# Token scaling on one core: seven token groups re-cut to one of 14 and six of 19, and the per-token weights brought in as long rows and spread to the partitions by TensorE transposes

## The chip, the cores and the metric

The kernel runs on 1 core of one Trainium2 chip. The metric is the device time of one execution in microseconds (us). Three executions of the kernel before were timed; the median counts.

## The reference, cut to what matters

```python
batch, seq, hidden, k = 16, 1024, 512, 2
x_expanded = x[:, :, np.newaxis, :].repeat(k, axis=2)      # x: (16, 1024, 512) float32
return x_expanded * expert_weights[..., np.newaxis]        # weights: (16, 1024, 2) float32
```

Each of 16,384 tokens has a row of 512 numbers and two weights. The output holds the row twice, once times each weight. The expert indices are not used. So 32 MiB are read, 64 MiB are written, and one multiplication is done for each number written. The weights are 128 KiB in all.

## The kernel before

The tokens are cut into seven groups. A group of T tokens per partition covers 128·T consecutive tokens, and partition p holds T consecutive tokens of it, so that a load of x moves one contiguous row of T·2 KB to each partition, and a store of the output one contiguous row of 4 KB for each token that it holds. The groups are 19, 19, 18, 18, 18, 18 and 18 tokens (line 30).

All x loads are issued from ScalarE's queue (line 77), all stores from SyncE's queue (line 117). There are two x buffers (`x_pool`) and three output buffers (`o_pool`). Each group is worked off in two halves (`halves`): the first takes the odd token, so 10 and 9 tokens or 9 and 9. For each half, `products` has VectorE multiply all tokens but the last in one instruction (line 85), with x broadcast over the two weights and the weights broadcast over the 512 numbers, while ScalarE does the two products of the last token (line 98). Then the half is stored. After both halves, the load of the group after next is issued, since it needs this group's x buffer. Group 0's x is loaded in its two halves, so that work can begin with the first; the others are loaded whole.

The weights lie in one tile, `w_tile`, 128 partitions by 256 numbers, for the whole kernel. They come by three DMAs (`weights`, line 50): group 0's from SyncE's queue, group 1's and then those of groups 2 to 6 together from ScalarE's queue, behind the two half loads of group 0 and ahead of the load of group 1. Each writes, for each partition and group, one run of T·2 numbers: 152 bytes for 19 tokens, 144 bytes for 18. That makes 128 + 128 + 640 = 896 such rows.

The order is the program's own (`manual_schedule`); nothing is reordered.

Of the kernel before, what the change touches and what calls it, by code (L numbers as in the profile page):

```python
# [1 line left out]

# [4 lines left out]


@with_exitstack
def kernel(  # L10
    ctx: ExitStack,
    tc: tile.TileContext,
    x: bass.AP,
    expert_indices: bass.AP,
    expert_weights: bass.AP,
    out: bass.AP,
):
    nc = tc.nc

    batch, seq, hidden = x.shape  # L20
    k = expert_weights.shape[-1]
    P = nc.NUM_PARTITIONS
    ntok = batch * seq
    assert ntok % P == 0

    f32 = mybir.dt.float32
    row = k * hidden


    groups = [19, 19, 18, 18, 18, 18, 18]  # L30
    assert sum(groups) * P == ntok
    TX = max(groups)
    TO = (TX + 1) // 2

    xf = x.rearrange("b s h -> (b s) h")
    of = out.rearrange("b s k h -> (b s) (k h)")
    wf = expert_weights.rearrange("b s k -> (b s) k")

    w_pool = ctx.enter_context(tc.tile_pool(name="w_pool", bufs=1))
    x_pool = ctx.enter_context(tc.tile_pool(name="x_pool", bufs=2))  # L40
    o_pool = ctx.enter_context(tc.tile_pool(name="o_pool", bufs=3))

    w_tile = w_pool.tile([P, sum(groups) * k], f32)

    def rows(flat, done, T):
        return flat[done * P : (done + T) * P, :].rearrange("(p a) n -> p (a n)", a=T)

    def weights(eng, head, G, T):
        lo = head * P
        eng.dma_start(  # L50
            out=w_tile[:, head * k : (head + G * T) * k].rearrange(
                "p (g n) -> p g n", g=G
            ),
            in_=wf[lo : lo + G * T * P, :].rearrange(
                "(g p a) n -> p g (a n)", g=G, p=P
            ),
        )

    ctx.enter_context(tc.manual_schedule())

    starts = [sum(groups[:i]) for i in range(len(groups))]
    loaded = []


    def halves(i):
        T = groups[i]
        return [T - T // 2, T // 2]

    def load(i):
        if i >= len(groups):  # L70
            return
        x_tile = x_pool.tile([P, TX * hidden], f32)
        loaded.append(x_tile)
        src = rows(xf, starts[i], groups[i])
        lo = 0
        for n in halves(i) if i == 0 else [groups[i]]:
            nc.scalar.dma_start(
                out=x_tile[:, lo * hidden : (lo + n) * hidden],
                in_=src[:, lo * hidden : (lo + n) * hidden],
            )  # L80
            lo += n

    def products(o_tile, x_tile, at, n, w_at):
        m = n - 1
        nc.vector.tensor_tensor(  # L85
            out=o_tile[:, : m * row].rearrange("p (t k h) -> p t k h", t=m, k=k),
            in0=x_tile[:, at * hidden : (at + m) * hidden]
            .rearrange("p (t h) -> p t h", t=m)
            .unsqueeze(2)
            .to_broadcast([P, m, k, hidden]),  # L90
            in1=w_tile[:, w_at : w_at + m * k]
            .rearrange("p (t k) -> p t k", t=m)
            .unsqueeze(3)
            .to_broadcast([P, m, k, hidden]),
            op=mybir.AluOpType.mult,
        )
        for c in range(m * k, n * k):
            nc.scalar.mul(  # L98
                out=o_tile[:, c * hidden : (c + 1) * hidden],
                in_=x_tile[:, (at + c // k) * hidden : (at + c // k + 1) * hidden],  # L100
                mul=w_tile[:, w_at + c : w_at + c + 1],
            )

    weights(nc.sync, 0, 1, groups[0])
    load(0)
    weights(nc.scalar, starts[1], 1, 19)
    weights(nc.scalar, starts[2], 5, 18)
    load(1)

    for i, T in enumerate(groups):  # L110
        x_tile = loaded[i]
        outr = rows(of, starts[i], T)
        at = 0
        for n in halves(i):
            o_tile = o_pool.tile([P, TO * row], f32)
            products(o_tile, x_tile, at, n, (starts[i] + at) * k)
            nc.sync.dma_start(  # L117
                out=outr[:, at * row : (at + n) * row], in_=o_tile[:, : n * row]
            )
            at += n  # L120
        load(i + 2)

# [1 line left out]
_INS = ['x', 'expert_indices', 'expert_weights']  # L124
_OUTS = [((16, 1024, 2, 512), 'float32')]


# [23 lines left out]
```

## Time and profile before

| | |
|---|---|
| timed runs | 239.56, 239.70, 240.71 us; median 239.7 us |
| the profiled execution | 239.73 us in all, span 237.9 us from first to last instruction |
| bytes moved by DMA | 100.80 MB, mean 424 GB/s over the span |
| VectorE busy | 123.7 us (52%), 14 instructions |
| ScalarE busy | 20.0 us (8%), 29 instructions |
| GpSimd busy | 0.2 us; TensorE is not used |
| DMA packets | 4112 |

Engines are named as in the profile: PE is TensorE, DVE is VectorE, ACT is ScalarE, POOL is GpSimd, SP is SyncE; ACTq and SPq are the queues from which DMAs are issued (q10 is ScalarE's, q1 SyncE's in the table of queues). In the views by window, the columns are the window, its length, each engine's busy time with its number of instructions, the granted TensorE clock, the mean busy share of the 16 DMA engines, and GB/s. A packet is counted whole in the window in which it starts, so a short window's share can be over 1.

### The profile page before, as it was taken

The numbers are of one execution on the slowest core, as the hardware profiler recorded it, in microseconds if no ns is written. First come the engines' busy times: TensorE is split into PE (matmuls) and PEld (weight loads), VectorE is DVE, ScalarE is ACT, GpSimd is POOL, SyncE is SP. The second block draws the span as 40 slices with busy tenths as digits, with TensorE's granted clock in tenths as the row PEclk, the third lists the DMA queues.
The fourth block names the chain that finished last, engine by engine and source line by source line (L and its number), as shares of the span: only waits on it lengthen the run. The fifth ranks groups of instructions, "written<-read, shape, count | busy, mean of one in ns | idle before, by whom it ended". The sixth has DMA issues, their size and how long they took to land.

```text
span 237.9 us, 159 instructions
## 1 busy us (share of the span) xinstructions
DVE 123.7 (52%) x14; ACT 20.0 (8%) x29; POOL 0.2 (0%) x4
## 2 busy tenths in 40 slices
DVE  0499659293193077950494900769505949680000
ACT  2220020100100020200202000202002020200000
POOL 0000000000000000000000000000000000000000
DMA  7999999999999999999999999999999999999996
GB/s 275 420 446 347 430 430 431 476 415 409 495 419 419 430 403 484 403 415 477 397 446 446 397 477 415 409 484 397 434 459 397 477 415 403 490 397 422 471 397 298
DMA packets 4112, 100.80 MB, mean 424 GB/s; under 512 B 1296, under 2 KB 1296, under 8 KB 1296
## 3 DMA queue, kind: packets, MB, share of 16 engines
q1 hardware_dynamic: 2160, 67.13, 65.4%
q10 hardware_dynamic: 1952, 33.67, 33.5%
HBM read 33.69 MB, written 67.11 MB: 424 GB/s over the span
## 4 chain that ended last, share of the span: by engine, by line
DMA 67%; DVE 22%; issue 0%; DVEq 0%; SPq 0%
DMA out_dram<-o_tile 63%; DVE o_tile L85 22%; DMA x_tile<-in_x_dram 4%; DVEq L85 0%; SPq L117 0%
## 5 line engine op out<-in xcount | busy, mean ns | idle before, releaser
L85 DVE TENSOR_TENSOR o_tile<-x_tile,w_tile 128x8192 f32<-128x8192 f32 (+1 forms) x14 | 123.7, 8844 | 89.4 <-DMA out_dram<-o_tile 75.4
L98 ACT ACTIVATE o_tile<-x_tile,w_tile 128x512 f32<-128x512 f32 x28 | 18.7, 714 | 181.7 <-DMA out_dram<-o_tile 157.4
L98 ACT ACT_TABLE_LOAD x1 | 1.3, 1283 | 4.2 <-DMA w_tile<-in_expert_weights_dram 4.2
L135 POOL MEMSET const-bfloat16-1.0<- 128x1 bf16 x1 | 0.1, 101 | 0.0
L135 POOL MEMSET const-uint8-127<- 128x1 uint8 x1 | 0.1, 101 | 0.0
L135 POOL MEMSET const-float32-0.0<- 128x1 f32 x1 | 0.1, 98 | 0.2 <-issue 0.2
L135 POOL MEMSET const-float32-1.0<- 128x1 f32 x1 | 0.1, 98 | 0.0
## 6 DMA issues: line engine op xcount, KB each, us to landing
out_dram<-o_tile SPq DMA_DIRECT2D x12, 4608.0 KB, 35.4
x_tile<-in_x_dram ACTq DMA_DIRECT2D x5, 4608.0 KB, 26.1
out_dram<-o_tile SPq DMA_DIRECT2D x2, 5120.0 KB, 34.8
x_tile<-in_x_dram ACTq DMA_DIRECT2D x1, 4864.0 KB, 29.5
x_tile<-in_x_dram ACTq DMA_DIRECT2D x1, 2560.0 KB, 8.8
x_tile<-in_x_dram ACTq DMA_DIRECT2D x1, 2304.0 KB, 13.9
w_tile<-in_expert_weights_dram ACTq DMA_DIRECT2D x1, 90.0 KB, 13.6
w_tile<-in_expert_weights_dram SPq DMA_DIRECT2D x1, 19.0 KB, 3.4
```

Source lines behind the costliest of these rows:

```text
L85: nc.vector.tensor_tensor(out=o_tile[:, : m * row].rearrange("p (t k h) -> p t k h", t=m, k=k), in0=x_tile[:, at * hidden : (at + m) * hidden]
L98: nc.scalar.mul(out=o_tile[:, c * hidden : (c + 1) * hidden], in_=x_tile[:, (at + c // k) * hidden : (at + c // k + 1) * hidden], mul=w_ti ...
L135: nc = _bacc.Bacc("TRN2", target_bir_lowering=False, num_devices=1)
```

## The change

The groups become 14, 19, 19, 19, 19, 19 and 19 tokens, so the first two stores hold 7 tokens each and all later ones 10 or 9. The number of x loads (8) and of stores (14) is the same.

The weights come in two DMAs (`weights_in`). One row of such a DMA is the weights of B = 8 partitions in a row: 8·14·2 numbers, 896 bytes, on 16 partitions for group 0; 8·19·2 numbers, 1216 bytes, on 96 partitions for the six other groups together. `weights_columns` then spreads them. For each of the 8 partitions r in a row, TensorE transposes that row's slice, so that tokens' weights lie on the partitions and (group, partition) on the free axis; VectorE copies the results out of PSUM, four slices at a time, in the order of the partitions; then TensorE transposes each group's 128 columns back, which gives 128 partitions by T·2 numbers, and `weights_out` copies these to `w_tile`. For group 0 that is 8 + 1 transposes and 2 + 1 copies, ahead of everything else on VectorE. For the other six groups it is 8 + 6 transposes and 2 + 1 copies; the two copies stand between VectorE's first and second product of group 0, the last one behind the second product. The transposes need an identity matrix, which GpSimd makes with a memset and an affine select.

```diff
-    groups = [19, 19, 18, 18, 18, 18, 18]
+    groups = [14, 19, 19, 19, 19, 19, 19]
...
+    B = 8
+    M = P // B
+    ident = w_pool.tile([P, P], f32)
+    nc.gpsimd.memset(ident, 0.0)
+    nc.gpsimd.affine_select(
+        out=ident,
+        in_=ident,
+        compare_op=mybir.AluOpType.not_equal,
+        fill=1.0,
+        base=0,
+        pattern=[[-1, P]],
+        channel_multiplier=1,
+    )
+
+    def weights_in(eng, head, G, T):
+        raw_tile = raw_pool.tile([G * M, B * T * k], f32, name=f"raw{T}_tile")
         eng.dma_start(
-            out=w_tile[:, head * k : (head + G * T) * k].rearrange(
-                "p (g n) -> p g n", g=G
+            out=raw_tile,
+            in_=wf[head * P : (head + G * T) * P, :].rearrange(
+                "(q a) n -> q (a n)", a=B * T
             ),
-            in_=wf[lo : lo + G * T * P, :].rearrange(
-                "(g p a) n -> p g (a n)", g=G, p=P
-            ),
+        )
+        return raw_tile
+
+    def weights_columns(raw_tile, G, T):
+        n = T * k
+        col_tile = raw_pool.tile([n, G * P], f32, name=f"col{T}_tile")
+        cols = col_tile.rearrange("c (q r) -> c q r", r=B)
+        for r0 in range(0, B, B // 2):
+            up_tile = psum.tile([n, B // 2, G * M], f32)
+            for r in range(B // 2):
+                nc.tensor.transpose(
+                    up_tile[:, r, :],
+                    raw_tile[:, (r0 + r) * n : (r0 + r + 1) * n],
+                    ident[: G * M, : G * M],
+                )
+            nc.vector.tensor_copy(
+                out=cols[:, :, r0 : r0 + B // 2],
+                in_=up_tile.rearrange("c r q -> c q r"),
+            )
+        down_tile = psum.tile([P, G * n], f32)
+        for g in range(G):
+            nc.tensor.transpose(
+                down_tile[:, g * n : (g + 1) * n],
+                col_tile[:, g * P : (g + 1) * P],
+                ident[:n, :n],
+            )
+        return down_tile
+
+    def weights_out(down_tile, head, G, T):
+        nc.vector.tensor_copy(
+            out=w_tile[:, head * k : (head + G * T) * k], in_=down_tile
         )
...
-    weights(nc.sync, 0, 1, groups[0])
+    raw_a = weights_in(nc.sync, starts[0], 1, 14)
     load(0)
-    weights(nc.scalar, starts[1], 1, 19)
-    weights(nc.scalar, starts[2], 5, 18)
+    raw_b = weights_in(nc.scalar, starts[1], 6, 19)
     load(1)
+    weights_out(weights_columns(raw_a, 1, 14), starts[0], 1, 14)
...
-        for n in halves(i):
+        for j, n in enumerate(halves(i)):
+            if i == 0 and j == 1:
+                down_b = weights_columns(raw_b, 6, 19)
             o_tile = o_pool.tile([P, TO * row], f32)
             products(o_tile, x_tile, at, n, (starts[i] + at) * k)
...
             at += n
+        if i == 0:
+            weights_out(down_b, starts[1], 6, 19)
         load(i + 2)
```

More of the change, by code (lines that the diff above doesn't have):

```diff
@@ L46, in rows @@
         return flat[done * P : (done + T) * P, :].rearrange("(p a) n -> p (a n)", a=T)
-    def weights(eng, head, G, T):
-        lo = head * P
+    B = 8
[13 more added lines that the diff above has]
+        raw_tile = raw_pool.tile([G * M, B * T * k], f32, name=f"raw{T}_tile")
         eng.dma_start(
-            out=w_tile[:, head * k : (head + G * T) * k].rearrange(
-                "p (g n) -> p g n", g=G
-            ),
-            in_=wf[lo : lo + G * T * P, :].rearrange(
-                "(g p a) n -> p g (a n)", g=G, p=P
-            ),
+            out=raw_tile,
+            in_=wf[head * P : (head + G * T) * P, :].rearrange(
+                "(q a) n -> q (a n)", a=B * T
+            ),
+        )
[22 more added lines that the diff above has]
+                ident[:n, :n],
+            )
+        return down_tile
+    def weights_out(down_tile, head, G, T):
+        nc.vector.tensor_copy(
+            out=w_tile[:, head * k : (head + G * T) * k], in_=down_tile
         )
```

3 lines of the change are left out of this document (added).

## The prediction

> **What bounds the kernel now.** I read the profile page first, for who is busy and what the chain that ended last is made of.
>
> ```profile
> span 237.9 us, 159 instructions
> DVE 123.7 (52%) x14; ACT 20.0 (8%) x29; POOL 0.2 (0%) x4
> DMA  7999999999999999999999999999999999999996
> DMA packets 4112, 100.80 MB, mean 424 GB/s; under 512 B 1296, under 2 KB 1296, under 8 KB 1296
> DMA out_dram<-o_tile 63%; DVE o_tile L85 22%; DMA x_tile<-in_x_dram 4%; DVEq L85 0%; SPq L117 0%
> ```
>
> No engine is busy for more than half the span, while the DMA line shows a 9 in every slice but the first and the last. The chain names VectorE's products with 22%, but DMA is full while they run, so that share is no bound. The waits say the same from the other side:
>
> ```profile
> ACT o_tile L98 <- DMA out_dram<-o_tile: 157.4, 11, 20.2
> DVE o_tile L85 <- DMA out_dram<-o_tile: 75.4, 11, 12.9
> DVE o_tile L85 <- DMA x_tile<-in_x_dram: 14.0, 2, 9.5
> ```
>
> Eleven of the fourteen products wait for an output buffer whose store has not landed. So I asked for the DMA rate by stretch:
>
> ```profile
> 1.90:2.60 0.70, 0.00 (x0) 0.00 (x0) 0.00 (x0) 1.00 0.64 189
> 4.50:9.00 4.50, 0.00 (x0) 0.96 (x1) 0.00 (x0) 1.00 1.00 430
> ...
> 15.40:22.00 6.60, 6.60 (x2) 1.06 (x2) 0.00 (x0) 1.00 1.01 413
> 24.50:213.00 188.50, 108.55 (x13) 16.01 (x24) 0.00 (x0) 1.00 1.00 432
> 213.00:236.90 23.90, 0.18 (x1) 0.00 (x0) 0.00 (x0) 1.00 0.97 420
> 236.90:237.90 1.00, 0.00 (x0) 0.00 (x0) 0.00 (x0) 1.00 0.00 0
> ```
>
> The middle 188.5 us run at 432 GB/s with a share of 1.00. At that rate 100.80 MB take 233.3 us. Nothing moves in the first 1.9 us or the last 1.0 us. 237.9 − 233.3 − 1.9 − 1.0 leaves 1.7 us that are lost near the start. The change moves the same x and output bytes, so these 1.7 us are all that it can win; the rest it could only lose. The profiled execution took 239.73 us, 1.83 us more than its span; the median is 239.7 us, so a difference in span can be taken from either.
>
> **The cost of small weight rows.** The weights are 896 rows of 144 or 152 bytes. Of the 1296 packets under 512 B the other 400 are what 25 DMAs leave at 16 each, and 4112 − 1296 = 2816 is 22 loads and stores of 128 rows. The window from 14.0 to 14.6 us, in which the second and third weight DMA run, gives the price of one:
>
> ```profile
> DMA packets 503, 0.19 MB, mean 309 GB/s; under 512 B 500, under 2 KB 500, under 8 KB 500
> q10 hardware_dynamic: 503, 0.19, 118.6%
> ```
>
> 118.6% of 16 engines for 0.6 us is 11.4 engine-us. Three of the packets are x rows of 38 KB, which at 432/16 = 27 GB/s take 1.44 us each, 4.3 together. The other 500 take 7.1, so 14.2 ns each. 896 of these are 12.7 engine-us, 0.80 us on each of 16 engines. This lies on the path, since the engines have no idle time to hide it.
>
> The change has 16 rows of 896 bytes and 96 of 1216, so 1 and 6 for each engine if the rows are spread evenly. I price each at 14.2 ns and its additional bytes at 27 GB/s: (896 − 146)/27 = 28 ns more, so 42 ns; (1216 − 146)/27 = 40 ns more, so 54 ns. 42 + 6 × 54 is 0.37 us for each engine. The gain is 0.80 − 0.37 = **0.43 us**. It could be 0.2 where small rows partly overlap their neighbours, as a share over 100% allows.
>
> At the start, 1.90 to 2.60 runs at 189 GB/s instead of 432, which loses 0.7 × 243/432 = 0.39 us. In it x's first rows and group 0's 128 weight rows start together, from two queues. The weight rows fall to 16. Between nothing (the queues ramp up by themselves) and 0.39 I take half, **0.2 us**.
>
> A rule speaks for more. The Trainium skill, "DMA: Bandwidth & Descriptors", section "Specifications", wants at least 512 bytes for line rate and says that below this the DMA engine does a read-modify-write. The row above gives 14.2 ns for a 146-byte row, 9 ns more than its bytes at 27 GB/s, so in the packet's own time the trace shows little of that; what is left of it would have to sit outside the records, which is the second rival below.
>
> **Tiles of 7, 10 and 9 tokens.** Loads stay 8 and stores 14, all of 128 rows, so the number of large rows stays 2816 and their bytes too: no change. Rows of 38 KB (x of 19 tokens) and 40 KB (10 tokens out) exist already in groups 0 and 1.
>
> **The work added on the engines** costs nothing as long as DMA never runs out of issued transfers. The one place where it might is the first stores.
>
> ```profile
> 0.72 0.89 ACTq L77 DMA_DIRECT2D x_tile<-in_x_dram  x2
> 0.72 0.37 SPq L50 DMA_DIRECT2D w_tile<-in_expert_weights_dram  x1
> 1.64 1.17 ACTq L50 DMA_DIRECT2D w_tile<-in_expert_weights_dram  x2
> 2.84 0.60 ACTq L77 DMA_DIRECT2D x_tile<-in_x_dram  x1
> 9.50 18.36 DVE L85 TENSOR_TENSOR o_tile<-x_tile,w_tile 128x9216 f32<-128x9216 f32 x2 [9.50 <-DMA x_tile<-in_x_dram]
> 19.35 194.23 SPq L117 DMA_DIRECT2D out_dram<-o_tile  x14
> ```
> ```profile
> L85 DVE TENSOR_TENSOR o_tile<-x_tile,w_tile 128x8192 f32<-128x8192 f32 x12 | 104.3, 8692 | 75.4 <-DMA out_dram<-o_tile 75.4
> L85 DVE TENSOR_TENSOR o_tile<-x_tile,w_tile 128x9216 f32<-128x9216 f32 x2 | 19.5, 9758 | 14.0 <-DMA x_tile<-in_x_dram 14.0
> L98 ACT ACTIVATE o_tile<-x_tile,w_tile 128x512 f32<-128x512 f32 x28 | 18.7, 714 | 181.7 <-DMA out_dram<-o_tile 157.4 <-DMA x_tile<-in_x_dram 24.3
> L135 POOL MEMSET const-float32-0.0<- 128x1 f32 x1 | 0.1, 98 | 0.2 <-issue 0.2
> ```
> ```profile
> x_tile<-in_x_dram ACTq DMA_DIRECT2D x1, 4864.0 KB, 29.5
> x_tile<-in_x_dram ACTq DMA_DIRECT2D x1, 2560.0 KB, 8.8
> w_tile<-in_expert_weights_dram ACTq DMA_DIRECT2D x1, 90.0 KB, 13.6
> w_tile<-in_expert_weights_dram SPq DMA_DIRECT2D x1, 19.0 KB, 3.4
> ```
>
> When the reads run out: the change first loads 14 + 19 tokens, 3584 + 4864 KB, and 128 KB of weights: 8576 KB or 8.78 MB, at 430 GB/s 20.4 us. From 1.9 us and 0.7 for the slow beginning, they end at 23.0. From issue (0.72) to first packets (1.9) it is 1.2 us, so the first store has to be issued by 21.8.
>
> When the first store is issued: its x is 1792 KB instead of 2560, 0.79 MB or 1.8 us less, so it is there at 9.50 − 1.8 = 7.7. Its weights land by 0.72 + 3.4 = 4.1. Then 9 transposes and 3 copies follow one another. No row shows TensorE; the nearest are a memset of one number per partition, 0.1 us, and an ACTIVATE of 512 numbers, 0.71. The pieces have 16 to 128 columns, so 12 × 0.1 = 1.2 us to 12 × 0.71 = 8.6 us; I take 0.3 us each, 3.6 us, since they lie between these two sizes and have hand-overs. The weights are then ready at 7.7 (5.3 to 12.7), about with x. GpSimd's two instructions for the identity, at 0.1 to 0.71 each, are done before the weights land. The product of 6 tokens has 6144 numbers; by (9758 − 8692)/1024 = 1.04 ns per number it takes 8692 − 2132 = 6560 ns. The store is issued at 14.3, at worst 19.3; before it was 19.35. The margin to 21.8 is 7.5, at worst 2.5 us.
>
> The second store: the two copies of group 1 to 6 stand on VectorE ahead of the second product, and that product, the second store and the load of group 2 (which waits for the buffer) queue behind them. The raw rows landed 13.6 us after an issue at 1.64 to 2.8, behind 4864 KB of x; behind 3584 KB it is 3.0 us sooner, by 13.4. Eight transposes at most 0.71 each: 19.1, mostly beside the first product. Two copies and 6.56 us: the store is issued at about 21.5, at worst 27.3. The reads and the first store (3.67 MB, 8.5 us) last to 31.5, so it is needed by 30.3. The six transposes back run beside that product, and the last copy delays group 1's product by under 0.71. Group 1's x lands at the latest with the 31.5, its product is done at 42, and by then the second store and group 2's load have put 20 us more in the queue. From there a group costs VectorE 9.76 + 8.69 = 18.5 us and DMA 14.94 MB, 34.6 us. On SP nothing but stores follows the weights; ScalarE issues one DMA less ahead of group 1's load, and finds the queue full either way. The end is as before: the last product has 9 tokens, and two stores are queued behind each other.
>
> Sum: 239.73 − 0.43 − 0.2 = **239.1 us**, a span of 237.3.
>
> **The rivals.** *Small rows cost more than their records show.* Then most of the 1.7 us goes, and about 1.5 with it: 238.2 us. For it: the low rate sits where small rows run, and the rule above. Against it: the same stretch holds the ramp of the queues and the first store's arrival, which stay.
>
> *Rows of 38 KB are slower.* In 15.4 to 22.0 only group 1's x is read, at 413 GB/s against 430 at 4.5 to 9.0. If that is the rows' own rate, five more such loads, 24.9 MB, take 60.3 instead of 57.9 us: 239.1 + 2.4 = 241.5 us. Against it: a packet is counted where it starts, and one round of 16 packets is 0.62 MB of the 2.7 in that window. It decides from a true rate under some 418 GB/s, where the loss is over 1.7 us.
>
> *The weights come too late and DMA starves.* If a step of the chain takes 1.5 us instead of 0.3, it ends at 4.1 + 18 = 22.1, the first store reaches the engines at 22.1 + 6.6 + 1.2 = 29.9 instead of by 23.0, and the time is 246. It begins to cost where the first product starts after 15.2. Against it: the bound from rows is 12.7.
>
> *The change does not do what it says:* the weight DMAs weigh as much as before, or were beside other work. Then it is 239.7, within the forecast's own side.
>
> **How the numbers follow.** About 0.5%, 1.2 us, is what can be told from no change: 238.5 to 240.9. The forecast with its bounds (gain of 0.2 to 0.8) and the rival of no effect have 0.76, all within; the faster rival 0.13; the two slower ones 0.07 and 0.04. So faster 0.13, same 0.76, slower 0.11. The range reaches from the faster rival, 238.2, to what one of the runs before reached, 240.7, with a part of the slow rows in it.
>
> **What would show it.** The profile after should have a 9 in all slices but the ends, 4112 − 896 + 112 − 16 = 3312 packets (one DMA less, so 384 under 512 B, and 112 more under 2 KB), the first product at about 7.7 (up to 12.7) and the first store at about 14.3, and 432 GB/s again from 24.5 on. The forecast is wrong if a stretch between 3 and 236 us shows DMA idle, if the rate with 38 KB rows falls below 430, or if the span shrinks by more than 1.2 us, which would say that small rows cost what their records do not show.

## The result: 1% slower, and the profile after

The changed kernel takes 242.67 us in the median of 19 runs (240.15 to 243.89), the kernel before 239.84 us (239.51 to 241.94, 19 runs). The ratio is 1.0093, 95% interval 1.0069 to 1.0117, from the comparisons, which leave disturbed runs out already. The forecast was 239.1 us, "same"; the range ended at 240.7. By the prediction's own bound of 0.5% this is slower, to which it gave a chance of 0.11. The profiled execution took 241.77 us, with a span of 240.0.

The page after, its span, its DMA lines and its chain:

```profile
span 240.0 us, 217 instructions
DMA  6998999999999999999999999999999999999992
GB/s 246 476 417 372 437 439 453 424 453 426 426 432 416 473 429 419 432 423 394 479 428 439 426 417 399 494 425 432 426 407 436 474 423 431 393 433 430 466 430 123
DMA packets 3312, 100.80 MB, mean 420 GB/s; under 512 B 384, under 2 KB 496, under 8 KB 496
DMA out_dram<-o_tile 64%; DVE o_tile L136 21%; DMA x_tile<-in_x_dram 3%; DVE col_tile L92 0%; DVEq L136 0%; SPq L170 0%
```

The packets are as worked out: 3312, 384 and 496. DMA is as full as before in all slices but one near the start and the ends, and the chain has the same members and, for under 1%, two copies of the weights. What differs is the last slice: 2 tenths and 123 GB/s, where before it was 6 tenths and 298.

The same stretches as in the prediction, in the changed kernel (engines PE, PEld, DVE, ACT, POOL, then clock, DMA share, GB/s):

```profile
1.90:2.60 0.70, 0.00 (x0) 0.00 (x0) 0.00 (x0) 0.00 (x0) 0.00 (x0) 1.00 0.65 131
4.50:9.00 4.50, 0.00 (x0) 0.00 (x0) 1.05 (x2) 0.89 (x1) 0.00 (x0) 1.00 1.00 424
15.40:22.00 6.60, 0.85 (x6) 0.71 (x6) 6.60 (x2) 0.00 (x0) 0.00 (x0) 1.00 1.00 413
24.50:213.00 188.50, 0.00 (x0) 0.00 (x0) 109.48 (x12) 16.01 (x24) 0.00 (x0) 1.00 1.00 432
213.00:236.90 23.90, 0.00 (x0) 0.00 (x0) 1.13 (x1) 0.00 (x0) 0.00 (x0) 1.00 0.96 416
```

The middle runs at 432 GB/s, as before. So the loss is at neither the rate nor the issue. It is in the last three microseconds. Before, then after, by single microseconds:

```profile
235.00:236.00 1.00, 0.00 (x0) 0.00 (x0) 0.00 (x0) 1.00 1.02 442
236.00:237.00 1.00, 0.00 (x0) 0.00 (x0) 0.00 (x0) 1.00 0.01 0
237.00:238.00 1.00, 0.00 (x0) 0.00 (x0) 0.00 (x0) 1.00 0.00 0
```
```profile
235.00:236.00 1.00, 0.00 (x0) 0.00 (x0) 0.00 (x0) 0.00 (x0) 0.00 (x0) 1.00 0.26 111
236.00:237.00 1.00, 0.00 (x0) 0.00 (x0) 0.00 (x0) 0.00 (x0) 0.00 (x0) 1.00 0.18 74
237.00:238.00 1.00, 0.00 (x0) 0.00 (x0) 0.00 (x0) 0.00 (x0) 0.00 (x0) 1.00 0.09 37
238.00:239.00 1.00, 0.00 (x0) 0.00 (x0) 0.00 (x0) 0.00 (x0) 0.00 (x0) 1.00 0.00 0
```

A packet counts where it starts. Before, the last rows start ahead of 236, and none after. In the changed kernel 74 GB/s for one microsecond is 74 KB, two rows of 36,864 bytes, and 37 is one row, between 237 and 238. Most of the 16 DMA engines have finished, while a few still have a row to move. The last store has landed only when the last engine is done.

The trace also has the time at which each of the 16 engines reports its share of a DMA as landed. In the change, thirteen engines have landed the last store by 236.75 us, two more by 237.8, and one at 239.16. For each kernel the table gives the first and the last of these times, from its profiled execution, with the time that the first store was issued. The variants, e1 to e15, are described below. The ratios go by the kernel before as it was timed beside each variant; its median there was 240.27 us (e1 to e4), 240.34 (e5 to e8), 239.87 (e9 to e11) and 240.39 (e12 to e15), so the medians of these four sets are not to be compared with each other.

| kernel | first store issued, us | first engine done, us | last engine done, us | median, us | ratio to before, 95% interval |
|---|---|---|---|---|---|
| before | 19.35 | 236.55 | 237.01 | 239.84 | |
| the change | 14.78 | 236.30 | 239.16 | 242.67 | 1.0093 (1.0069 to 1.0117) |
| e1, new groups alone | 14.46 | 236.20 | 239.50 | 242.43 | 1.0074 (1.0039 to 1.0110) |
| e2, long weight rows alone | 19.42 | 236.30 | 236.65 | 240.58 | 1.0008 (0.9979 to 1.0037) |
| e3, 20 and six 18, long rows | 19.46 | 236.33 | 237.59 | 240.19 | 1.0000 (0.9976 to 1.0025) |
| e4, 20 and six 18, small rows | 19.60 | 236.41 | 237.54 | 240.09 | 1.0004 (0.9984 to 1.0023) |
| e5, six 19, then 14 | 19.13 | 236.42 | 236.87 | 239.77 | 0.9994 (0.9952 to 1.0035) |
| e6, 14 first, then even | 14.43 | 236.48 | 238.15 | 242.01 | 1.0062 (1.0026 to 1.0098) |
| e7, stores of 10 and 8 | 19.41 | 236.39 | 239.17 | 240.78 | 1.0021 (0.9987 to 1.0056) |
| e8, change, group 0 as 10 and 4 | 19.41 | 236.02 | 237.34 | 240.86 | 1.0029 (0.9997 to 1.0061) |
| e9, change, first store held | 18.94 | 236.01 | 240.07 | 240.85 | 1.0024 (0.9990 to 1.0059) |
| e10, before, group 0 as 7, 6, 6 | 14.36 | 236.70 | 240.77 | 243.04 | 1.0084 (1.0046 to 1.0122) |
| e11, before, first store held | 23.80 | 236.32 | 237.65 | 240.82 | 1.0027 (0.9991 to 1.0064) |
| e12, change, one queue | 15.17 | 236.66 | 241.07 | 243.08 | 1.0099 (1.0061 to 1.0138) |
| e13, before, one queue | 19.97 | 236.71 | 239.90 | 242.50 | 1.0065 (1.0037 to 1.0092) |
| e14, 7, 6, 6 and held | 18.70 | 236.53 | 239.48 | 241.25 | 1.0035 (1.0007 to 1.0063) |
| e15, long weight rows, one queue | 19.75 | 236.85 | 239.78 | 242.79 | 1.0089 (1.0056 to 1.0123) |

In every kernel the first engine is done between 236.0 and 236.9 us, and the span ends 0.81 to 0.99 us after the last engine. What differs is how far the last engine lags: 0.46 us before, 2.86 us in the change. The 2.1 us by which the span grew are this lag (2.4 us more) less 0.25 us by which the first engine ended sooner. A single execution says little of a kernel, since the lag differs from run to run (before ranges from 239.51 to 241.94, and the profiled executions of e9 and e14, 242.67 and 242.24 us, are among the longest of theirs); the ratios and intervals carry the comparisons below.

### The profile page after: what moved, and what is told of

The parts are those of the page before. It is cut to its first block, busy times and chain, and to the rows that moved or that the text cites. A ratio compares the mean times of both kernels' runs of the same rounds, so it can differ in the third digit from the quotient of the medians.

```text
span 240.0 us, 217 instructions
## 1 busy us (share of the span) xinstructions
PE 3.0 (1%) x23; PEld 2.2 (1%) x23; DVE 125.4 (52%) x20; ACT 20.0 (8%) x29; POOL 0.7 (0%) x6
## 2 busy tenths in 40 slices
DMA packets 3312, 100.80 MB, mean 420 GB/s; under 512 B 384, under 2 KB 496, under 8 KB 496
## 4 chain that ended last, share of the span: by engine, by line
DMA 67%; DVE 21%; issue 0%; DVEq 0%; SPq 0%
DMA out_dram<-o_tile 64%; DVE o_tile L136 21%; DMA x_tile<-in_x_dram 3%; DVE col_tile L92 0%; DVEq L136 0%; SPq L170 0%
## 5 line engine op out<-in xcount | busy, mean ns | idle before, releaser
L136 DVE TENSOR_TENSOR o_tile<-x_tile,w_tile 128x9216 f32<-128x9216 f32 (+2 forms) x14 | 123.7, 8842 | 84.6 <-DMA out_dram<-o_tile 73.2
L92 DVE COPY col_tile<-up_tile 28x64 f32<-28x64 f32 (+1 forms) x4 | 1.3, 374 | 3.8 <-PE up_tile L87 3.8
L87 PE MATMUL up_tile<-ident,raw_tile 16*28 16x16 f32 (+1 forms) x16 | 1.8, 269 | 12.1 <-DMA raw_tile<-in_expert_weights_dram 12.1
L87 PEld LDWEIGHTS up_tile<-ident,raw_tile 16*28 16x28 f32 (+1 forms) x16 | 1.3, 119 | 12.3 <-issue 12.2
L98 PE MATMUL down_tile<-ident,col_tile 38*128 38x38 f32 (+1 forms) x7 | 1.2, 305 | 1.4 <-DVE col_tile L92 1.4
L98 PEld LDWEIGHTS down_tile<-ident,col_tile 38*128 38x128 f32 (+1 forms) x7 | 0.9, 208 | 1.9 <-DVE col_tile L92 1.9
L106 DVE COPY w_tile<-down_tile 128x28 f32<-128x28 f32 (+1 forms) x2 | 0.6, 284 | 0.4 <-PE down_tile L98 0.4
```

Source lines behind the costliest of these rows:

```text
L87: nc.tensor.transpose(up_tile[:, r, :], raw_tile[:, (r0 + r) * n : (r0 + r + 1) * n], ident[: G * M, : G * M],)
L92: nc.vector.tensor_copy(out=cols[:, :, r0 : r0 + B // 2], in_=up_tile.rearrange("c r q -> c q r"),)
L98: nc.tensor.transpose(down_tile[:, g * n : (g + 1) * n], col_tile[:, g * P : (g + 1) * P], ident[:n, :n],)
L106: nc.vector.tensor_copy(out=w_tile[:, head * k : (head + G * T) * k], in_=down_tile)
L136: nc.vector.tensor_tensor(out=o_tile[:, : m * row].rearrange("p (t k h) -> p t k h", t=m, k=k), in0=x_tile[:, at * hidden : (at + m) * hidden]
```

## The experiments

**Which half of the change?** The groups were changed without the weights (e1), and the weights without the groups (e2).

```diff
e1, in the kernel before:
-    groups = [19, 19, 18, 18, 18, 18, 18]
+    groups = [14, 19, 19, 19, 19, 19, 19]
...
-    weights(nc.scalar, starts[1], 1, 19)
-    weights(nc.scalar, starts[2], 5, 18)
+    weights(nc.scalar, starts[1], 6, 19)
e2, in the changed kernel (columns and copies likewise):
-    groups = [14, 19, 19, 19, 19, 19, 19]
+    groups = [19, 19, 18, 18, 18, 18, 18]
...
-    raw_b = weights_in(nc.scalar, starts[1], 6, 19)
+    raw_c = weights_in(nc.scalar, starts[1], 1, 19)
+    raw_b = weights_in(nc.scalar, starts[2], 5, 18)
```

> The changed groups (14 and six times 19) with the three-row-size small weight DMAs of before (two DMAs, rows of 112 and 152 bytes). Theory P (the group cut makes DMA engines drift apart: its stores alternate between rows of 40 and 36 KB and its loads have 38 KB, where before nearly all rows had 36 KB, so an engine that falls behind stays behind and the last store ends on one late engine): slow like the change, 241.5 to 243 us (ratio 1.007 to 1.013), one or a few engines with their last packets 1 to 3 us after the others. Theory W (the long weight rows upset the start, 16 rows on 16 engines and 6 each, and the spread seeded there stays): like before, 239.5 to 240.3 us, all engines ending within 0.7 us.

> The groups of before (19, 19, five times 18) with the weights in long rows and TensorE transposes (rows of 1216, 1216 and 1152 bytes). Theory P (group cut): like before or 0.3 to 0.6 us less, 239.1 to 239.8 us, engines ending within 0.7 us. Theory W (weight rows): slow like the change, 241.5 to 243 us, a late engine at the end.

e1 is as slow as the change, 1.0074, and e2 is like before, 1.0008 with an interval that reaches to both sides. So theory W falls: the groups do it, and the weights show neither harm nor gain. The end of e1 and that of e2, in the same single microseconds:

```profile
236.00:237.00 1.00, 0.00 (x0) 0.00 (x0) 0.00 (x0) 1.00 0.26 111
237.00:238.00 1.00, 0.00 (x0) 0.00 (x0) 0.00 (x0) 1.00 0.34 147
```
```profile
236.00:237.00 1.00, 0.00 (x0) 0.00 (x0) 0.00 (x0) 0.00 (x0) 0.00 (x0) 1.00 0.01 0
237.00:238.00 1.00, 0.00 (x0) 0.00 (x0) 0.00 (x0) 0.00 (x0) 0.00 (x0) 1.00 0.00 0
```

e1 has rows left that start after 237 us, with small weight rows; e2 has none after 236, with long ones.

**Long against small weight rows with even groups** (e3 and e4: 20 and six times 18; otherwise as the changed kernel, and as the kernel before).

> Groups of 20 and six times 18, so all halves equal (10 and 10, then 9 and 9; rows of 36 KB for nearly all loads and stores), with the weights in long rows and transposes. Theory P: 239.0 to 239.8 us, the engines together at the end. Theory W: 241.5 to 243 us. A third theory, F (it is the early first store of the group of 14, with x rows of 14 KB, that upsets the engines): like before here, and slow in the run with the groups alone.

> Groups of 20 and six times 18 with the small weight rows of before. Theory P and F: like before, 239.5 to 240.2 us. Theory W: like before too. Beside the run with the long rows it gives the price of the small rows by itself: 0.43 us by the prediction.

Both are like before (1.0000 and 1.0004). They are 0.1 us apart, by the medians the wrong way round and by the ratios the right way, so the 0.43 us of the small rows can't be seen here, nor ruled out. The long rows are not worth over about 0.5 us, the edge of e2's interval (0.21% of 239.8).

**Unequal rows through the run, or the early first store?** The new groups have two properties: stores of 40 and 36 KB rows beside loads of 38 KB, and a first group so small that its first store comes at 14.8 us. e5 keeps the first and takes away the second, e6 the reverse; e7 adds unequal stores to the kernel before; e8 gives the changed kernel's first store 10 tokens.

```diff
e5, in the kernel before (weights cut likewise):
-    groups = [19, 19, 18, 18, 18, 18, 18]
+    groups = [19, 19, 19, 19, 19, 19, 14]
e6, in the kernel before (weights cut likewise):
-    groups = [19, 19, 18, 18, 18, 18, 18]
+    groups = [14, 20, 20, 20, 18, 18, 18]
e7, in the kernel before:
-        return [T - T // 2, T // 2]
+        return [10, T - 10]
e8, in the changed kernel:
-        return [T - T // 2, T // 2]
+        return [10, 4] if i == 0 else [T - T // 2, T // 2]
```

> Six groups of 19 and 14 last, small weight rows. The first two groups, the first store and the x loads beside it are those of before; from the third group on loads have rows of 38 KB and stores of 40 and 36 KB. Theory P (unequal rows make engines drift apart through the run): 241.5 to 243 us. Theory F (the first store of a small first group comes at 15 us, in the middle of the x loads, and seeds the lag): like before, 239.5 to 240.5 us.

> Groups of 14, 20, 20, 20, 18, 18, 18, small weight rows: the small first group of the change, but all halves equal and loads and stores of one row size in each group (40 KB, then 36 KB). Theory P: like before, 239.5 to 240.5 us. Theory F: 241.5 to 243 us.

> The kernel before with its 18-token groups stored as 10 and 8 tokens instead of 9 and 9 (rows of 40 and 32 KB; loads stay 36 KB). Theory P: slower than before by 1 to 3 us. Theory F: like before, 239.5 to 240.5 us.

> The changed kernel with group 0 cut into 10 and 4 tokens instead of 7 and 7, so that the first store is issued at about 19.3 us as before, not at 14.8; all else stays. Theory F: 239.5 to 240.5 us, like before. Theory P: 241.5 to 243 us, as the change.

e5, the same seven sizes with the 14 at the end, is like before (0.9994); e6, with even halves but 14 first, is slow (1.0062). That is theory F and against P. e7 is not distinguishable from before (1.0021). e8 falls from 1.0093 to 1.0029, a little above what F expected in the median, 240.86 us. The rows of 38 KB, one of the prediction's rivals, are cleared by e5 as well: it has five such loads where before has one and the change six, no loss, and this rate in the middle:

```profile
24.50:213.00 188.50, 105.77 (x13) 16.01 (x24) 0.00 (x0) 1.00 1.00 433
```

**Is it the time of the first store, or the small pieces?** In e9 and e11 VectorE does the product of the first four tokens twice, which holds the first store back by 4.2 to 4.5 us. What VectorE does behind it, the other stores of group 0 and the load of group 2 come as much later too. e10 cuts the 19 tokens of group 0 of the kernel before into 7, 6 and 6, so that its first store comes early; e14 is e10 with the store held back.

```diff
e9, e11 and e14:
+            if i == 0 and at == 0:
+                twice(o_tile, x_tile, 0)
             products(o_tile, x_tile, at, n, (starts[i] + at) * k)
e10 and e14, in the kernel before:
-        return [T - T // 2, T // 2]
+        return [7, 6, 6] if i == 0 else [T - T // 2, T // 2]
```

> The changed kernel, in which VectorE does the product of the first four tokens of the first tile twice (4096 numbers, about 4.3 us), so that the first store is issued at about 19.1 us instead of 14.8; nothing else differs. Theory F1 (the time of the first store, in the middle of the x loads, makes an engine late): back to 239.5 to 240.8 us, near before. Theory F2 (it is the small group itself, its 14 and 28 KB rows): stays at 242 to 243 us.

> The kernel before with group 0 (19 tokens) loaded and stored as 7, 6 and 6 tokens instead of 10 and 9: the first store is issued at about 14.5 us, with one load and one store more. Theory F1: slower than before by 1.5 to 2.5 us, 241.5 to 243. Theory F2 (a small group): like before, 239.5 to 240.5.

> The kernel before with the same doubled product: the first store is issued at about 23.6 us instead of 19.35, shortly before the reads run out at about 26. Theory F1: like before or with fewer late engines, 239.5 to 239.9 us median, and 240.5 to 242 if the reads run out first. Theory F2: like before.

> The kernel before with group 0 loaded and stored as 7, 6 and 6 tokens and the product of the first four tokens done twice, so that the first store is issued at about 18.8 us instead of 14.4. Theory F1 (the time of the first store): 239.7 to 241 us, 2 us less than with the three pieces alone. Theory F2 (small pieces at the start): 242.4 to 243.5, as with the three pieces alone.

The timelines of SyncE's queue in e10, e9 and e14 show that the stores of group 0 moved as a whole, with the distance between them as it was (in the change the two begin at 14.78 and take 7.70):

```profile
14.36 11.11 SPq L117 DMA_DIRECT2D out_dram<-o_tile  x3
```
```profile
18.94 7.71 SPq L187 DMA_DIRECT2D out_dram<-o_tile  x2
```
```profile
18.70 11.11 SPq L134 DMA_DIRECT2D out_dram<-o_tile  x3
```

Making the first store early in the kernel before costs 0.84%, 2 us (e10; by the medians of its set it is 3.2 us). Holding it back takes most of the loss away in both: 1.0093 to 1.0024 in the changed kernel, with intervals that do not overlap, and 1.0084 to 1.0035 in the cut one, where they do. VectorE does 4.4 us more work in these faster kernels. F1 carries the larger part, though e9, e10 and e14 each came out up to 0.25 us above the range that it gave, and e11 0.9 us above. Each pair spans two sets, so its two ratios go by different timings of the kernel before. Of what moves with the first store, the load of group 2 does not look like the cause: e8 issues it at 23.59 us, 1.4 us later than the change, and is rid of most of the loss, while e10 issues it at 25.16 and is slow. That the small pieces have a part of their own, some 0.25%, is possible: e8, e9 and e14 all lie between 1.0024 and 1.0035, but only e14's interval is clear of 1. Holding back further does not help: e11, which has no small pieces and its first store at 23.8 us, is 1.0027, with an interval from 0.9991 to 1.0064.

The end of e10, whose late engines still begin rows between 238 and 239:

```profile
236.00:237.00 1.00, 0.00 (x0) 0.00 (x0) 0.00 (x0) 1.00 0.35 148
237.00:238.00 1.00, 0.00 (x0) 0.00 (x0) 0.00 (x0) 1.00 0.17 74
238.00:239.00 1.00, 0.00 (x0) 0.00 (x0) 0.00 (x0) 1.00 0.26 111
```

**Why does an engine fall behind?** A thought was that each DMA engine serves a row of the load queue and a row of the store queue in turn, and that this lets them part. In e12, e13 and e15 all DMAs are issued from SyncE's queue, in the same program order.

```diff
-            nc.scalar.dma_start(
+            nc.sync.dma_start(
...
-    raw_b = weights_in(nc.scalar, starts[1], 6, 19)
+    raw_b = weights_in(nc.sync, starts[1], 6, 19)
```

> The changed kernel with its x loads and raw weights issued from SyncE's queue too, in the same program order, so that each DMA engine serves loads and stores one DMA after another and not a row of each in turn. Theory Q (an engine falls behind where it has two queues to serve in turn): no late engine, 238.8 to 239.6 us, faster than the change by about 3 us. Theory M (it falls behind because some engines read while others write, whatever the queue): 241.5 to 243 us, as the change. If DMA ran out of issued work, over 243.

> The kernel before with all DMAs on SyncE's queue, same program order. Theory Q: 239.3 to 239.7 us in nearly all runs, without the runs of 241 to 242 that before has. Theory M: like before, 239.5 to 242 us.

> The groups of before, the weights in long rows with transposes, all DMAs on SyncE's queue: a candidate to beat both. By theory Q 238.9 to 239.4 us, before less the 0.4 us of the small rows; by theory M 239.5 to 242 us.

Theory Q falls. e12 takes 243.08 us (1.0099, 1.0061 to 1.0138), e13 242.50 us (1.0065, 1.0037 to 1.0092), e15 242.79 us (1.0089, 1.0056 to 1.0123). One queue makes the kernel before slow too. DMA does not run out; in e13 the middle runs at 431 GB/s and the end shows a late engine, as in the change:

```profile
24.50:213.00 188.50, 106.19 (x13) 16.00 (x24) 0.00 (x0) 1.00 1.00 431
...
236.00:237.00 1.00, 0.00 (x0) 0.00 (x0) 0.00 (x0) 1.00 0.26 111
237.00:238.00 1.00, 0.00 (x0) 0.00 (x0) 0.00 (x0) 1.00 0.00 0
238.00:239.00 1.00, 0.00 (x0) 0.00 (x0) 0.00 (x0) 1.00 0.09 37
```

By the landing times of e13's DMAs, the engines are 0.5 us apart at 85 us, 1.35 at 96, 2.4 at 130 and 3.2 at the end. There the lag is not one event but grows in steps. That would fit theory M, that an engine which reads while the others write, or the reverse, loses more; but M expected e13 and e15 within 239.5 to 242 us, and both are slower. It stays open.

One thing that the traces do show is how the first store meets the loads. Before, then the change:

```profile
22.00:23.00 1.00, 1.00 (x1) 0.00 (x0) 0.00 (x0) 1.00 1.42 389
23.00:24.00 1.00, 1.00 (x1) 0.00 (x0) 0.00 (x0) 1.00 0.00 0
24.00:25.00 1.00, 1.00 (x1) 0.00 (x0) 0.00 (x0) 1.00 1.51 655
```
```profile
17.00:18.00 1.00, 0.00 (x0) 0.00 (x0) 1.00 (x1) 0.00 (x0) 0.00 (x0) 1.00 1.44 545
18.00:19.00 1.00, 0.00 (x0) 0.00 (x0) 1.00 (x1) 0.00 (x0) 0.00 (x0) 1.00 0.18 68
19.00:20.00 1.00, 0.00 (x0) 0.00 (x0) 1.00 (x1) 0.00 (x0) 0.00 (x0) 1.00 1.10 469
```

Before, no row starts on any engine for a whole microsecond: in the packet records the 38 KB rows then under way take 2.1 to 2.4 us instead of 1.44, on all 16 engines, and all engines go on together. In the change rows do start in that time, and those under way take up to 0.4 us longer, each by another amount. It is tempting to say that the common hold keeps the engines together, but the traces speak against it. In e11 the first store's rows start at 26.1 us as the loads end, no row is held, and the engines land group 1's load within 0.6 us of each other. In e9 only some rows are held, by up to 0.4 us, and the engines land that load within 0.54 us.

Nor is the lag of the change there from the first store on. At 30 us its engines land group 1's load 2.2 us apart (before, at 32 us, 0.5), but up to a row of the store, 1.06 us, of this can be the order in which an engine took its two queues. At 87 us, when stores alone have been under way for some ten us, they are 1.1 us apart (before, in such a stretch at 95, 0.5). At 124, again with stores alone, they are 2.8 apart, as at the end. In between the load issued at 85.83 us begins beside the stores, and single rows are slow: one store row of 40 KB that starts at 89.0 takes 2.4 us where others take 1.51, and two rows of the load at 107 and 108 take 0.5 and 0.6 us more than their 1.44. In e1 four store rows that start at 88.7 to 89.1 take 3.0 us, and its engines go from 0.8 us apart at 87 to 3.1 at 124; e10 has four such rows, of 2.5 to 2.6 us, at 67.4. After 26 us, before, e2, e3, e4 and e5 have no row of 28 KB or more that takes over 0.5 us more than is usual for its size and queue, and theirs are the smallest lags of all, 0.35 to 1.26 us; each of the other kernels has three or more. So the lag of these executions is made in the middle of the run; that the slow rows make it is likely, and not shown. How the time of the first store bears on them stays open: e9 and e14, with the store held, have such rows too.

## Why the prediction was wrong, point by point

The step that failed is the one that costed the earlier first store at nothing: "The work added on the engines costs nothing as long as DMA never runs out of issued transfers", and with it "The end is as before". DMA did not run out, and the times in that part lay within their bounds or ahead of them: the first product started at 8.13 us (forecast 7.7, up to 12.7), the first store was issued at 14.78 (14.3, up to 19.3), as this part of the timeline after and the line for SyncE's stores show.

```profile
3.44 0.29 PEld L87 LDWEIGHTS up_tile<-ident,raw_tile 16*28 16x28 f32 x8 [3.44 <-issue]
...
4.51 0.19 DVE L106 COPY w_tile<-down_tile 128x28 f32<-128x28 f32 x1 [0.40 <-PE down_tile L98]
8.11 1.28 ACT L149 ACT_TABLE_LOAD   x1 [8.11 <-DMA x_tile<-in_x_dram]
8.13 6.56 DVE L136 TENSOR_TENSOR o_tile<-x_tile,w_tile 128x6144 f32<-128x6144 f32 x1 [3.44 <-DMA x_tile<-in_x_dram]
...
14.78 7.70 SPq L170 DMA_DIRECT2D out_dram<-o_tile  x2
```

But the argument treated the 16 DMA engines as one resource that is either full or idle, and took "DMA busy" for "all engines level". A store lands when its last engine is done, so the end is set by the slowest engine, and what sets its lag is not seen in the mean rate. The store that came 4.6 us earlier was counted as nothing but margin, 7.5 us of it; it cost about 2 us, by the ratios of e10 and of the change, and held back in the changed kernel (e9) most of that is gone. None of the rivals had this mechanism. The two that end on the slower side, 241.5 and 246 us, both fell, the first though its time was the nearest to the 242.67 measured: the rows of 38 KB run at the full rate (e5), and the weights were ready at 4.7 us, not late.

The 1.0 us at the end, in which nothing moves, stood as a constant of the sum. It is the term that was mis-sized: from the first engine done to the end of the span it is 1.3 us before and 3.7 us after, 0.5 and 2.9 of them the lag.

The gain of 0.43 us by the longer rows is not refuted and not shown: e2 leaves room for at most 0.5 us, and the pair e3 and e4 shows 0.1 us one way or the other. In the profiled executions the first engine of the change is done 0.25 us sooner than before. The 0.2 us at the start did not appear: 1.90 to 2.60 ran at 131 GB/s, before at 189. The rival that small rows cost far more than their records show, with a gain of 1.5 us, is excluded by e2. The Trainium skill ("DMA: Bandwidth & Descriptors", "Specifications") names a read-modify-write below 512 bytes; whatever it costs here lies within e2's 0.5 us, about what the 14.2 ns of each row already hold.

The chain of the first weights took 1.26 us from the first transpose to the last copy (3.44 to 4.70), 0.1 us for each of its 12 steps, the low end of the 1.2 to 8.6 us bounds and not the 3.6 us that I took. The error did not show in the time of the first store, since x came last, 0.4 us later than forecast.

## What to carry to other kernels

Where DMA is full from end to end, look at when each DMA engine finishes, not only at the mean rate: the last slice of the DMA line and a count of rows that start in the last microseconds show a lagging engine at once. A product or a store that is ready earlier is not free there. The time of the first stores alone was worth up to 0.9% in this kernel, so an edit of the first tiles should be timed by itself, as was done here with a held-back copy of the same kernel. None of the fifteen variants ran beyond doubt faster than the kernel before.

## What the runs showed of the hardware that was not expected

- The 16 DMA engines of a core can end a saturated run 0.35 us apart (e2) or 4.4 us (e12), with the same bytes and nearly the same rate in the middle (433 and 432 GB/s); the first of them ended between 236.0 and 236.9 us in all kernels.
- Putting loads and stores on one queue instead of two, in the same order, cost 0.65% (e13).
- The first store held up the rows of all 16 engines by 0.7 to 0.9 us in the kernel before, and by nothing to 0.4 us in the change.
- Single large rows took up to twice their usual time (3.0 us for 1.51, in four rows at 89 us in e1), some 3 us after a load was issued beside running stores.
